# Merged 512-column matmuls, paired rotary scores and a later-ordered second input in a two-layer decoder kernel

## The chip, the cores and the metric

The kernel runs on one core of one Trainium2 chip. The metric is the time of one execution in device microseconds (us); a time without further words is the median of several runs. A profile is one execution, recorded by the hardware profiler. The engines are TensorE (PE in the rows; its weight loads, PEld, overlap its matmuls), VectorE (DVE), ScalarE (ACT), GpSimd (POOL) and SyncE (SP), which here only issues DMAs.

## The reference: what is computed

256 tokens of width 1024 pass two layers; everything is float32.

```python
for i in range(DEPTH):                                   # DEPTH = 2
    hn = rms_norm(h, attn_norm[i])
    if i < N_A_LAYERS:                                   # layer 0
        mix = diff_attention(hn, positions, ...)         # 8 heads, q and k as 2 x 64, v 128, T5 bias
    else:                                                # layer 1
        k_nope, k_pe, v = shared_latent_kv(h, positions, ...)
        mix = mla_attention(hn, ..., k_nope, k_pe, v)    # 16 heads
    h = h + mix
    h = h + conv_gated_ffn(rms_norm(h, ffn_norm[i]), ...)
    h = h + per_layer_embedding(h, p[i], ...)

def mla_attention(...):                                  # one block of 128 queries
    sc = (einsum('bqhd,bkhd->bhqk', qn, k_nope)          # d = 128, per head
          + einsum('bqhr,bkr->bhqk', qp, k_pe)) * scale  # r = 64, one rotary key for all heads
    a = softmax(where(causal_mask, sc, NEG_INF))
    return einsum('bhqk,bkhv->bqhv', a, v)

def conv_gated_ffn(h, w_in, conv_w, conv_b, w_out):      # d_ff = 2816 = 22 x 128
    a, g = split(causal_conv3(h @ w_in) + conv_b)
    return (silu(g) * a) @ w_out
```

The latent key and value come from `rms_norm(h, kv_norm) @ w_dkv` (256 + 64 wide), the queries from `hn @ w_dq` (512 wide) and then `w_uq`.

## The kernel before

**Pairs of numbers.** Each float32 operand is held as a high part and a low part in a shorter format. A product is three matmuls into one accumulator, high times high, high times low and low times high: `mm3`, L199, L200 and L201. The first operand of `T.matmul` (`lhsT`) is the stationary 128x128 tile, the second (`rhs`) the moving one, and its width is the width in columns that the text speaks of. The parts are made by `split`: the high part by ScalarE (L205, or L208 with a gain), the low part by VectorE (L206 or L209).

**Weights.** They lie in units of 128x1024 floats (512 KB) in the order in which they are used. `fetch` (L228) brings a unit by a DMA of SyncE into one of five `st` buffers, `split_unit` casts the high part on ScalarE (L246) and takes the low part on VectorE or on POOL (L247); `share[0]` is the fraction that goes to POOL. The two results stand in a ring of four pairs, `wh` and `wl` (`BUF_W = 4`, L76). A pair is free again when the last matmul that reads it is through.

**Two forms of projection.** In the attentions (`block`, L376) the tokens are stationary: a tile of 128 tokens times 256 columns of a weight unit, for both token tiles (t = 0, 1) into two halves of one accumulator bank of 512 floats. In the feed-forward stages (`wst`, L637) the weight block is stationary and the 256 tokens move, so an output tile is the transposed residual's; `add_h` (L628, L635) adds it. In the second feed-forward product the operand `g`, the gated activation, stands in tiles `og` and `qk` of high and low parts, four or two of them beside each other.

**The stages of the profile.** Start and first block, to some 20 us; layer 0's attention with its projections (`proj_a`, `attn_a`, to 140 us) and output product (to 165); its feed-forward products (165 to 284 and 284 to 345); its embedding (`ple`, to some 378); the second attention's latent (`lps`, 320 columns, then the rotary key `kp`), its query latent (`dps`, 512 columns) to 394; its heads (to 545); the second feed-forward network (560 to 690 and 690 to 752) and the embedding.

**The second attention's input.** The last output tile of `ple` goes through VectorE and ScalarE (`evac`, L844 to L846) and gets the residual added (L628). `b_post` then splits each tile with the latent's gain into `kvs["kvH"]`, `kvs["kvL"]`. The same residual with the attention's own gain is split into `hgH`, `hgL` after `lps` is written out.

**The scores of the second attention** (`s1`, one head at a time, L1155 on): per 128 queries three matmuls of the nope part and three of the rotary part. The rotary queries of two heads lie in the rows 0 to 63 and 64 to 127 of one tile; the rotary key is held twice, each time padded with zeros in the other half (`kpH[e]`), so that each rotary matmul runs over all 128 rows.

**What sets the order.** The program is written as generators: `weave` runs the attention's steps between the projections by an estimate of TensorE's time (`clk`), and `later` delays a step by such an estimate. A scheduler then orders each engine's queue by a simulation of the whole, with priorities that follow the written order; `tc.high_priority` and `tc.issue_after` bend it. Accumulator banks come from four pools A, T, B and C; `BANKS_B` (L80) names, item by item, the pool that a projection of the second attention takes.

## Time and profile before

| | us |
|---|---|
| median of 3 runs | 778.34 |
| lowest and highest of them | 777.44, 778.69 |
| the profiled execution's own time | 777.55 |
| its span | 775.8 |
| TensorE busy | 753.3 |
| VectorE busy | 570.8 |
| ScalarE busy | 485.1 |
| POOL busy | 272.7 |

The span runs from the first to the last instruction of the profiled execution; the rest of its own time, 1.75 us, lies around it. A row of the page or of a group gives line, engine, operation, the output and input tiles by the program's names, the shapes and the count, then busy time and the mean of one in ns, then the idle time of that engine ahead of them with what ended it. A timeline row gives the start in us, the duration, engine, line, tiles and count, and in brackets an idle time ahead of it with its releaser. Matmuls are pipelined: the time of a step is the distance between two starts, and the duration of a row is longer. A row of the table by stretch gives the stretch, its length, the busy time of each engine (and its instructions), the granted clock of TensorE (1.00 is the full one of its two levels), the DMA engines' share and GB/s.

### The profile page before, as it was taken

Reading aid. Unit: us, or ns where it says so; the run is one execution under the profiler, and the core shown is the slowest. Engines: PE = TensorE matmul, PEld = TensorE weight load, DVE = VectorE, ACT = ScalarE, POOL = GpSimd, SP = SyncE. Lnnn points to the kernel's source line nnn. Section 1 sums busy time; section 2 is a strip of 40 time slices with the busy share of each in tenths; the row PEclk is TensorE's granted clock in tenths of the full one; section 3 lists DMA queues with packets and bytes.
Section 4 is the critical chain, followed back from the end, with each engine's and each line's share of the span. In section 5 each row is a group of like instructions: output and inputs, shape, how many; then the busy total and the mean of one; then the engine's idle time right before and its main releaser. Section 6 shows DMA issues by size and latency. Waiting matters only on the chain.

```text
span 775.8 us, 16482 instructions
## 1 busy us (share of the span) xinstructions
PE 753.3 (97%) x6396; PEld 740.0 (95%) x6396; DVE 570.8 (74%) x1141; ACT 485.1 (63%) x1044; POOL 272.7 (35%) x187
## 2 busy tenths in 40 slices
PE   7999999999999999999898999999999999999996
PEld 6999989999999999999798999999999999999996
DVE  6677888568997796546788887876688778875545
ACT  6537876676566665447766876564676666655442
POOL 2655464232332511115616555221342332201231
PEclk9999999999999999999999999999999999999999
DMA  8994444256665576655354133344465566565531
GB/s 293 278 234 160 134 150 136 82 187 181 195 190 177 181 230 216 190 165 176 117 164 166 43 98 112 108 136 135 138 191 189 170 185 195 187 185 174 187 108 55
DMA packets 37519, 127.97 MB, mean 165 GB/s; under 512 B 4672, under 2 KB 6208, under 8 KB 37440
## 3 DMA queue, kind: packets, MB, share of 16 engines
q1 hardware_dynamic: 36432, 126.29, 52.5%
q8 instruction: 50, 0.82, 0.4%
q10 hardware_dynamic: 1008, 0.63, 0.3%
q14 instruction: 29, 0.24, 0.1%
HBM read 125.75 MB, written 1.15 MB: 164 GB/s over the span
## 4 chain that ended last, share of the span: by engine, by line
PE 82%; DVE 8%; ACT 4%; POOL 3%; issue 2%; DMA 1%; SPq 0%; POOLq 0%; ACTq 0%; DVEq 0%
PE pa L199 17%; PE pa L200 17%; PE pa L201 17%; PE pc L201 8%; PE pc L200 8%; PE pc L199 8%; DVE wl L247 2%; POOL wl L247 1%; DVE og L209 1%; ACT wh L246 1%; PE pt L193 1%; POOL s L280 1%; PE pb L482 1%; PE pb L549 1%; PE pc L193 1%
## 5 line engine op out<-in xcount | busy, mean ns | idle before, releaser
L246 ACT CAST wh<-st 128x1024 fp32r<-128x1024 f32 x221 | 230.8, 1049 | 166.5 <-issue 61.2
L247 DVE TENSOR_TENSOR wl<-st,wh 128x1024 fp32r<-128x1024 f32 x160 | 204.6, 1280 | 99.4 <-ACT wh L246 95.8
L247 POOL TENSOR_TENSOR wl<-st,wh 128x1024 fp32r<-128x1024 f32 x61 | 149.6, 2452 | 224.9 <-ACT wh L246 200.2
L201 PE MATMUL pa<-hgH,wl 128*128 128x256 f32 x496 | 140.7, 284 | 0.4 <-POOL wl L247 0.4
L199 PE MATMUL pa<-hgH,wh 128*128 128x256 f32 x496 | 140.4, 283 | 0.0
L200 PE MATMUL pa<-hgL,wh 128*128 128x256 f32 x496 | 140.3, 283 | 0.0
L200 PE MATMUL pa<-og,wh 128*128 128x256 f32 x352 | 99.8, 284 | 0.9 <-DVE og L209 0.9
L199 PE MATMUL pa<-og,wh 128*128 128x256 f32 x352 | 100.2, 288 | 0.1
L201 PE MATMUL pa<-og,wl 128*128 128x256 f32 x352 | 100.1, 285 | 0.0
L199 PE MATMUL pa<-wh,hgH 128*128 128x256 f32 x328 | 93.5, 289 | 4.8 <-DVE d L361 1.7
L304 POOL TENSOR_TENSOR ssq<-ssq,d 128x256 f32<-128x256 f32 x35 | 37.1, 1059 | 172.8 <-ACT d L303 172.4
L201 PE MATMUL pc<-hgH,wl 128*128 128x256 f32 x336 | 95.6, 285 | 1.0 <-DVE wl L247 1.0
L201 PEld LDWEIGHTS pa<-hgH,wl 128*128 128x128 f32 x496 | 95.2, 192 | 0.6 <-POOL wl L247 0.6
L200 PE MATMUL pc<-hgL,wh 128*128 128x256 f32 x336 | 95.1, 283 | 0.1
L199 PEld LDWEIGHTS pa<-hgH,wh 128*128 128x128 f32 x496 | 95.1, 192 | 0.1
L200 PEld LDWEIGHTS pa<-hgL,wh 128*128 128x128 f32 x496 | 95.1, 192 | 0.1
L199 PE MATMUL pc<-hgH,wh 128*128 128x256 f32 x336 | 95.0, 284 | 0.0
L200 PE MATMUL pa<-wl,hgH 128*128 128x256 f32 x328 | 93.4, 286 | 1.5 <-DVE wl L247 0.8
L201 PE MATMUL pa<-wh,hgL 128*128 128x256 f32 x328 | 93.1, 286 | 0.1
L200 PEld LDWEIGHTS pa<-og,wh 128*128 128x128 f32 x352 | 67.7, 192 | 1.1 <-DVE og L209 1.1
L199 PEld LDWEIGHTS pa<-wh,hgH 128*128 128x128 f32 x328 | 62.0, 191 | 6.9 <-DVE d L361 1.9
L199 PEld LDWEIGHTS pa<-og,wh 128*128 128x128 f32 x352 | 67.2, 192 | 0.8 <-ACT og L208 0.3
(304 smaller groups left out, 1913.6 us busy)
## 6 DMA issues: line engine op xcount, KB each, us to landing
st<-in_wall SPq DMA_DIRECT2D x225, 512.0 KB, 3.6
oh<-s SPq DMA_DIRECT2D x24, 128.0 KB, 6.6
hT<-in_x SPq DMA_DIRECT2D x4, 256.0 KB, 5.1
st<-in_wall SPq DMA_DIRECT2D x4, 256.0 KB, 5.3
st<-in_xn SPq DMA_DIRECT2D x2, 512.0 KB, 7.2
d<-in_p SPq DMA_DIRECT2D x2, 256.0 KB, 4.7
out_h<-hT SPq DMA_DIRECT2D x4, 128.0 KB, 1.9
out_h<-hT ACTq DMA_DIRECT2D x4, 128.0 KB, 1.9
```

The source lines that it names most:

```text
L193: lastmm[0] = T.transpose(o, i, ident).ins
L199: T.matmul(ps, lhsT=aH, rhs=bH, start=start, stop=False)
L200: T.matmul(ps, lhsT=aH, rhs=bL, start=False, stop=False)
L201: lastmm[0] = T.matmul(ps, lhsT=aL, rhs=bH, start=False, stop=stop).ins
L209: V.scalar_tensor_tensor(lo, src, scale, f(hi), ALU.mult, ALU.subtract)
L246: A.copy(hi, st)
L247: eng.tensor_sub(lo, st, f(hi))
L280: G.tensor_tensor(dst, src, neghalf[:, :n], ALU.pow)
L304: sqlast[0] = G.tensor_add(sq, sq, t).ins
L482: T.matmul(ps[:, i * 32:(i + 1) * 32], lhsT=lh, rhs=tb[z], start=z == 0, stop=z == 2)
L549: T.matmul(pss[e][:, a:b], lhsT=x[rows, j, t * P:(t + 1) * P], rhs=y[rows, j, :b - a], start=start, stop=stop)
```

## The change

**512 columns in the second feed-forward product.** The high and low parts of `g` now stand side by side, and a new `mm2` multiplies the stationary high part of the weight with both at once, one matmul of 512 columns, then the low part of the weight with the high part, 256 columns, into the first half of the bank. The second half is added to the residual by VectorE ahead of the first. Seven of eight output tiles go this way; the last keeps `mm3`.

**512 columns in the projections.** Query and key weights of the first attention's pairs of heads are laid side by side in one 512-column unit, as are key and value weights of the second, and the rotary queries of four heads beside the nope queries of two of them (`pq_b`). `wide` runs them with one token tile per bank. All four units of a query-key block are held through both token tiles. The order of the second attention's items, its banks and the place from which POOL gets a share are new.

**Rotary scores.** The scores of two heads are computed together. The rotary matmuls use the 64 rows of their own head, written in alternation, the key stands once, and the zeros, POOL's fill and copies are gone.

**The second attention's input.** The splits with the attention's own gain wait for the last split of the latent's input; the last evacuation of the first `ple` has high priority; POOL takes no low parts from there until later.

**The first block.** It now has four units with two halves each, and 512 columns a matmul.

The diff, cut:

```diff
-    order = [("kv", 0), ("kv", 1), ("pe", 0), ("qn", 0), ("qn", 1), ("kv", 2), ("qn", 2), ("pe", 1)]
-    for p in range(3, 8):
-        order += [("kv", p)] + ([("pe", p // 2)] if p % 2 == 0 else []) + [("qn", p)]
-    order.insert(order.index(("qn", 6)) + 1, ("wo", (0, 4)))
+    order = [("kv", 0), ("kv", 1), ("pq", 0), ("qn", 1), ("kv", 2), ("pq", 1), ("kv", 3), ("qn", 3)]
+    for p in range(4, 8):
+        order += [("kv", p), ("qn", p) if p % 2 else ("pq", p // 2)]
+    order.insert(order.index(("pq", 3)) + 1, ("wo", (0, 4)))
...
-BANKS_B = "ABACAACAACAA"
+BANKS_B = "ABACBACACCAA"
 SH_A = 0.5
 SH_FFN = 0.4
 SH_PLE = 0.5
-SH_B0 = 0.5
...
+    def mm2(ps, aH, aL, b, start, stop):
+
+
+        n = b.shape[-1]
+        clk[0] += 3 * max(0.107, n * 0.000427)
+        T.matmul(ps[:, :2 * n], lhsT=aH, rhs=b.rearrange("p c n -> p (c n)"), start=start, stop=False)
+        lastmm[0] = T.matmul(ps[:, :n], lhsT=aL, rhs=b[:, 0], start=False, stop=stop).ins
...
+    for i in range(4):
+        nc.sync.dma_start(hT[:, 2 * i:2 * i + 2], xT[:, 2 * i:2 * i + 2])
+        for st in fetch(2):
+            pass
         first.append(st)
...
+    def wide(t, units, lH, lL, ps):
+
+        for i, u in enumerate(units):
+            for j in range(2):
+                k, c = 2 * i + j, slice(j * 512, (j + 1) * 512)
+                mm3(ps, lH[:, k, t * P:(t + 1) * P], lL[:, k, t * P:(t + 1) * P], u[0][:, c], u[1][:, c], k == 0,
+                    k == 2 * len(units) - 1)
...
+            us = [load_unit() for i in range(4)]
+            for t in range(NT):
                 ps = bankA()
-                us = [(load_unit(), 4) for i in range(2)]
-                block(8, us, S, 0, S, hgH, hgL, ps)
-            yield 1
-            todo.append((s, ps))
-            if p == 0 and s == 0:
-                epsx()
...
+        for s in range(2):
+            later(LAG, lambda s=s, pr=(qk(), qk()): fin(s, *pr))
+        us = [load_unit() for i in range(2)]
+        ps = bankA()
+        block(8, [(u, 4) for u in us], S, 0, S, hgH, hgL, ps)
+        yield 1
+        dH, dL = qk(), qk()
+        for t in range(NT):
+            split(dH[:, t], dL[:, t], ps[:, t * S:(t + 1) * S], xs["r"][:, t:t + 1])
+        QA[p]["v"] = dH, dL
...
-    def add_h(n, ps, post):
+    def add_h(n, ps, post, more=None):
 
         if post:
+            if more is not None:
+                V.tensor_add(hT[:, n], hT[:, n], more)
...
-            mm3(pss[n], u[0][:, b * P:(b + 1) * P], u[1][:, b * P:(b + 1) * P], bH(k), bL(k), k == 0, k == kn - 1)
+                pss[n] = bank()
+            ps, c, p = pss[n], slice(z * P, (z + 1) * P), b(k)
+            if n < wide:
+                mm2(ps, u[0][:, c], u[1][:, c], p, k == 0, k == kn - 1)
+            else:
+                mm3(ps[:, :S], u[0][:, c], u[1][:, c], p[:, 0], p[:, 1], k == 0, k == kn - 1)
             if k == kn - 1:
-                add_h(n, pss.pop(n), post)
-            if b == 7:
+                add_h(n, ps[:, :S], post, ps[:, S:] if n < wide else None)
+                del pss[n]
...
-        run(wst(FFN_OUT_ORDER, lambda k: gH[k], lambda k: gL[k], post, bankW))
+        run(wst(FFN_OUT_ORDER, lambda k: g[k], post, bankW, NK - 1))
...
-                if n == 4:
+                if n == 4 and l == 1:
...
-                evac(*todo.pop(0))
+                if n == NK - 2 and l == 0:
+                    with tc.high_priority():
+                        evac(*todo.pop(0))
+                else:
+                    evac(*todo.pop(0))
...
-        split(kvs["kvH"][n // 4][:, n % 4], kvs["kvL"][n // 4][:, n % 4], ps, col(C_KV + n))
+        kvs["last"] = split(kvs["kvH"][n // 4][:, n % 4], kvs["kvL"][n // 4][:, n % 4], ps, col(C_KV + n))
...
-    share[0] = SH_B0
+    share[0] = 0.0
...
-        split(kvs["hgH"][n // 4][:, n % 4], kvs["hgL"][n // 4][:, n % 4], hT[:, n], col(C_ATTN[1] + n))
-    zer = d_tile(S)
-    G.memset(zer, 0.0)
-    with tc.issue_after(sqlast[0]):
-        for tl in (kpH, kpL):
-            G.tensor_copy(tl[0][64:, :], zer[64:, :])
-            G.tensor_copy(tl[1][:64, :], zer[:64, :])
+        with tc.issue_after(kvs["last"][0]), tc.issue_after(kvs["last"][1]):
+            split(kvs["hgH"][n // 4][:, n % 4], kvs["hgL"][n // 4][:, n % 4], hT[:, n], col(C_ATTN[1] + n))
...
         u = load_unit()
-        ps = bankF()
-        block(2, [(u, 2)], 512, 0, S, ckH, ckL, ps)
-        yield 1.3
-        src = norm_block(ps, 2, P, EPS)
-        ps = bankF()
-        block(2, [(u, 2)], 512, S, S, ckH, ckL, ps)
-        yield 1.3
+        pss = [bankF() for t in range(NT)]
+        for t in range(NT):
+            wide(t, [u], ckH, ckL, pss[t])
+        yield 2.6
...
+    def pq_b(c):
...
+        us = [load_unit() for i in range(2)]
+        pss = []
+        for t in range(NT):
+            pss.append(bankF())
+            wide(t, us, cqH, cqL, pss[t])
+            yield 2.6
+        qn = norm_block(pss, 4, 64, EPS)
+        q_fin(2 * c, norm_block([x[:, S:] for x in pss], 2, P, EPS))
...
+            pss = [bankB() for _ in range(2)]
+
+            def nope(t, a, b, start):
+                for e in range(2):
+                    ts_ = slice(t * P, (t + 1) * P)
+                    mm3(pss[e][:, a:b], q[0][:, e, ts_], q[1][:, e, ts_], k[0][:, e, :b - a], k[1][:, e, :b - a],
+                        start, not start)
+
+            def rotary(t, a, b, start):
+                for z, (x, y) in enumerate(((pe[0], kpH), (pe[0], kpL), (pe[1], kpH))):
+                    for e in range(2):
+                        rows = slice(e * 64, e * 64 + 64)
+                        lastmm[0] = T.matmul(pss[e][:, a:b], lhsT=x[rows, p % 2, t * P:(t + 1) * P],
+                                             rhs=y[rows, :b - a], start=start and z == 0,
+                                             stop=not start and z == 2).ins
+                clk[0] += 0.36
+
+            nope(*QR[0], True)
+            rotary(*QR[0], False)
+            rotary(*QR[1], True)
+            nope(*QR[1], False)
+            for e in range(2):
...
-            if n == 6:
+            if n == 7:
...
-        for s in range(3):
-            natural(wqkv[:, s * 1024 + p * 256:s * 1024 + (p + 1) * 256], 4)
+        q, k, v = (wqkv[:, s * 1024 + p * 256:s * 1024 + (p + 1) * 256] for s in range(3))
+        natural(np.concatenate([q, k], axis=1), 2)
+        natural(v, 4)
...
+    def pq(c):
+        natural(np.concatenate([uq[:, 4 * c:4 * c + 4, P:].reshape(512, 256), qn(2 * c)], axis=1), 2)
...
```

The order in which the instructions stand, at three places. In the second feed-forward product of layer 0 on TensorE, `og` and `qk` hold the activation pair, `wh` and `wl` the weight unit's parts (the rows with `hgH`, `hgL` are the end of the first product); before:

```order
L200 MATMUL pc_4070<-hgL_2344,wh_4103 128x256
L201 MATMUL pc_4070<-hgH_2343,wl_4104 128x256
L199 MATMUL pa_4167<-og_2604,wh_4163 128x256
L200 MATMUL pa_4167<-og_2605,wh_4163 128x256
L201 MATMUL pa_4167<-og_2604,wl_4164 128x256
```

and in the changed kernel, at the change from one output tile to the next:

```order
L207 MATMUL pa_4005<-qk_3795,wh_4085 128x512
L208 MATMUL pa_4005<-qk_3795,wl_4086 128x256
L207 MATMUL pa_4005<-qk_3869,wh_4085 128x512
L208 MATMUL pa_4005<-qk_3869,wl_4086 128x256
L207 MATMUL pc_4103<-og_2407,wh_4085 128x512
L208 MATMUL pc_4103<-og_2407,wl_4086 128x256
```

Two rows stand where three stood. Over the whole queue of TensorE 6373 matmuls become 5681; 256-column ones fall from 5476 to 4092 and 512-column ones rise from 48 to 740.

On TensorE in the second attention's scores, `hgH` and `hgL` are the rotary queries' tiles, `peH` and `peL` the rotary key's, `qk` the nope parts, `pb` the head's bank; before, one head:

```order
L199 MATMUL pb_5882<-hgH_5226,peH_5675 128x128
L200 MATMUL pb_5882<-hgL_5227,peH_5675 128x128
L201 MATMUL pb_5882<-hgH_5226,peL_5676 128x128
L199 MATMUL pb_5882<-qk_5569,qk_5726 128x256
L200 MATMUL pb_5882<-qk_5570,qk_5726 128x256
L201 MATMUL pb_5882<-qk_5569,qk_5727 128x256
L199 MATMUL pb_5882<-hgH_5226,peH_5675 128x256
L200 MATMUL pb_5882<-hgL_5227,peH_5675 128x256
L201 MATMUL pb_5882<-hgH_5226,peL_5676 128x256
```

and in the changed kernel the first pair of heads, and the first head of the second pair:

```order
L1187 MATMUL pb_5494<-hgH_4882,peH_5335 128x128
L1187 MATMUL pb_5495<-hgH_4882,peH_5335 128x128
L1187 MATMUL pb_5494<-hgL_4883,peH_5335 128x128
L1187 MATMUL pb_5495<-hgL_4883,peH_5335 128x128
L192 MATMUL pt_5480<-ident_109,d_5384 128x128 x4
L1187 MATMUL pb_5494<-hgH_4882,peL_5336 128x128
L1187 MATMUL pb_5495<-hgH_4882,peL_5336 128x128
...
L1187 MATMUL pb_5542<-hgH_4882,peH_5335 128x128
L1187 MATMUL pb_5542<-hgL_4883,peH_5335 128x128
L1187 MATMUL pb_5542<-hgH_4882,peL_5336 128x128
L1187 MATMUL pb_5542<-hgH_4882,peH_5335 128x256
```

Seven of the eight pairs of heads alternate like the first, and in three of these another instruction (here four transposes) stands between; one pair has all six of a head behind one another.

On VectorE at the end of layer 0's embedding, `pc` is the last output tile, `rb` the row factor, `prj` the projected embedding, `hT` the residual, and `og` the split tiles of the second attention's two inputs; before:

```order
L844 TENSOR_TENSOR pc_5141<-pc_5141,rb_4991 128x256
L209 SCALAR_TENSOR_TENSOR og_5034<-hT_82,cst_83,og_5032 128x256 x2
L209 SCALAR_TENSOR_TENSOR og_5035<-hT_82,cst_83,og_5033 128x256 x2
L846 TENSOR_TENSOR pc_5141<-pc_5141,prj_2272 128x256
L628 TENSOR_TENSOR pc_5141<-pc_5141,hT_82 128x256
L209 SCALAR_TENSOR_TENSOR og_5031<-pc_5141,cst_83,og_5029 128x256
L247 TENSOR_TENSOR wl_5415<-st_5412,wh_5414 128x1024
```

and in the changed kernel:

```order
L865 TENSOR_TENSOR pc_4797<-pc_4797,rb_4647 128x256
L251 TENSOR_TENSOR wl_5047<-st_5044,wh_5046 128x1024
L867 TENSOR_TENSOR pc_4797<-pc_4797,prj_2075 128x256
L650 TENSOR_TENSOR pc_4797<-pc_4797,hT_82 128x256
L214 SCALAR_TENSOR_TENSOR og_4687<-pc_4797,cst_83,og_4685 128x256
L214 SCALAR_TENSOR_TENSOR og_4690<-hT_82,cst_83,og_4688 128x256 x4
L214 SCALAR_TENSOR_TENSOR og_4691<-hT_82,cst_83,og_4689 128x256 x2
L251 TENSOR_TENSOR wl_5065<-st_5062,wh_5064 128x1024
```

The four splits of `hT` have gone from ahead of the last tile's own steps to behind its split, and a weight's low part has come between. Of the low parts of all weights VectorE has 165 in place of 160, and POOL 54 in place of 61.

## Rows read from the trace of the kernel before

**Rows 1.** The page: busy time of each engine, and the chain by engine.
```profile
PE 753.3 (97%) x6396; PEld 740.0 (95%) x6396; DVE 570.8 (74%) x1141; ACT 485.1 (63%) x1044; POOL 272.7 (35%) x187
...
PE 82%; DVE 8%; ACT 4%; POOL 3%; issue 2%; DMA 1%; SPq 0%; POOLq 0%; ACTq 0%; DVEq 0%
```

**Rows 2.** Busy time by stretch (from:to, length, engines, clock, DMA).
```profile
0.00:20.00 20.00, 15.96 (x96) 13.01 (x97) 13.85 (x51) 13.39 (x27) 5.95 (x15) 1.00 0.83 296
60.00:140.00 80.00, 78.32 (x728) 74.76 (x727) 68.02 (x175) 59.84 (x170) 38.14 (x24) 0.98 0.44 139
284.00:345.00 61.00, 61.00 (x514) 61.00 (x513) 35.53 (x45) 31.28 (x50) 8.09 (x6) 1.00 0.61 192
394.00:432.00 38.00, 34.22 (x280) 32.90 (x278) 30.29 (x56) 26.53 (x80) 15.80 (x10) 1.00 0.46 149
```

**Rows 3.** Timeline of TensorE, 200 to 204 us, first feed-forward product.
```profile
199.75 0.28 PE L199 MATMUL pa<-hgH,wh 128*128 128x256 f32 x1
...
203.59 0.28 PE L201 MATMUL pa<-hgH,wl 128*128 128x256 f32 x1
```

**Rows 4.** Timeline of TensorE, 380 to 396 us, second attention's query latent.
```profile
385.33 0.39 PE L200 MATMUL pc<-wl,og 128*128 128x512 f32 x1
...
391.72 0.39 PE L201 MATMUL pc<-wh,og 128*128 128x512 f32 x1
```

**Rows 5.** The group of line 635, from the groups by tile hT.
```profile
L635 DVE TENSOR_TENSOR hT<-hT,pa x40: 394/416/425, 119.5 to 541.4; 128x256 f32<-128x256 f32 x40
```

**Rows 6.** Timeline of TensorE, 500 to 505 us, one head's rotary scores.
```profile
502.86 0.28 PE L199 MATMUL pb<-hgH,peH 128*128 128x128 f32 x1
...
503.19 0.33 PE L199 MATMUL pb<-qk 128*128 128x256 f32 x1
...
503.61 0.28 PE L199 MATMUL pb<-hgH,peH 128*128 128x256 f32 x1
...
503.96 0.22 PE L201 MATMUL pb<-qk 128*128 128x128 f32 x1
```

**Rows 7.** Timeline of TensorE, first attention: scores on half height, two places.
```profile
65.41 0.95 PE L549 MATMUL pb<-qk 64*128 64x128 f32 x6
66.29 0.39 PE L200 MATMUL pa<-wl,hgH 128*128 128x256 f32 x1
...
70.69 0.28 PE L200 MATMUL pa<-wl,hgH 128*128 128x256 f32 x1
70.90 0.96 PE L549 MATMUL pb<-qk 64*128 64x128 f32 x12
71.78 0.39 PE L201 MATMUL pa<-wh,hgL 128*128 128x256 f32 x1
72.01 0.60 PE L193 MATMUL pt<-ident,d 128*128 128x128 f32 x4
```

**Rows 8.** Timeline of TensorE, 376 to 383 us, end of the embedding.
```profile
377.86 0.28 PE L201 MATMUL pa<-dr,xl 128*128 128x256 f32 x1
380.93 0.42 PE L199 MATMUL pb<-wh,og 128*128 128x320 f32 x1 [2.78 <-ACT og L208]
```

**Rows 9.** Timeline of ScalarE, the same place.
```profile
378.94 1.56 ACT L735 COPY prj<-pa 128x512 f32<-128x512 f32 x3 [2.78 <-DVE pc L846]
380.38 0.50 ACT L208 ACTIVATE og<-pc,cst 128x256 fp32r<-128x256 f32 x1
```

**Rows 10.** Timeline of VectorE, the same place.
```profile
373.81 4.75 DVE L209 SCALAR_TENSOR_TENSOR og<-hT,cst,og 128x256 fp32r<-128x256 f32 x4
378.49 0.42 DVE L846 TENSOR_TENSOR pc<-pc,prj 128x256 f32<-128x256 f32 x1
```

**Rows 11.** The page, costliest groups: the weights' splits.
```profile
L246 ACT CAST wh<-st 128x1024 fp32r<-128x1024 f32 x221 | 230.8, 1049 | 166.5 <-issue 61.2
L247 DVE TENSOR_TENSOR wl<-st,wh 128x1024 fp32r<-128x1024 f32 x160 | 204.6, 1280 | 99.4 <-ACT wh L246 95.8
L247 POOL TENSOR_TENSOR wl<-st,wh 128x1024 fp32r<-128x1024 f32 x61 | 149.6, 2452 | 224.9 <-ACT wh L246 200.2
```

233 lines of the change are left out of this document (103 added, 130 removed).

## The prediction

> **What bounds the kernel now.** I read the busy times of the page first, then busy time by stage, then single rows of TensorE's timeline for the price of one matmul, then the three engines around one wait. The page says that TensorE is busy for 753.3 of 775.8 us with 6396 instructions, and that the chain of work that ended last runs on it for 82% [rows 1]. The stages agree: in a second feed-forward product TensorE is busy for 61.00 of 61.00 us, with VectorE at 35.53 [rows 2]. The second such stage (690 to 752 us) is alike. There only fewer or shorter matmuls shorten the time. In the attentions TensorE is nearly full too, 78.32 of 80 us in the middle of the first one and 34.22 of 38 us at the front of the second, but VectorE is at 68.02 (85%) and 30.29 us (80%) there [rows 2]. So a microsecond saved on TensorE is worth a microsecond in the feed-forward stages, and perhaps less in the attentions.
>
> **Merged matmuls.** Total columns stay the same: one 512-column matmul stands where two 256-column ones with the same stationary tile stood. By the order, 6373 matmuls become 5681, 692 fewer: 2 x 7 x 22 = 308 in the two feed-forward products (seven of eight output tiles), 4 x 8 x 2 x 3 = 192 in the query and key projections of the first attention, 96 in kv and 96 in pq of the second (8 units x 2 k x 2 t x 3, and 4 x 4 x 2 x 3). The price of a 256-column matmul: from 199.75 to 203.59 us 32 steps pass, 3.84 us, 120 ns a step [rows 3]. Of a 512-column one: from 385.33 to 391.72 us, 28 steps of 6.39 us, 228 ns [rows 4]. Two steps become one: 240 - 228 = 12 ns, at about 11 ns where the 256-column step is 119 ns, as in the projections. 308 x 11.8 + 384 x 11 ns = 3.6 + 4.2 = 7.9 us. All of it is on TensorE, and the feed-forward part is on the path that sets the end. The 512-column rows come from the first projection of the second attention, where the wide operand is a weight; that the wide operand is an activation pair in the new product I take to cost nothing more, since a row names no such difference.
>
> The Trainium skill ("TensorE: Matmul & The Clock Gate", Back-to-back issue gap) gives the step as columns divided by 2.4 plus 2.5 ns, so that a merge would save 2.5 ns. By that, 692 merges would save an estimated 1.7 us in place of the 7.9. The trace does not agree: its 120 and 228 ns leave a fixed part of 12 ns, and the sum goes by the rows.
>
> The new product leaves one half to be added, 14 more adds on VectorE at 416 ns [rows 5], 5.8 us. They lie in stages where VectorE is idle for 25 of 61 us [rows 2] and the last output tile is not merged, so the tail gets none: cost nil. If that cover were gone, 5.8 us would be the most.
>
> **Rotary scores.** Per pair of heads the kernel before runs 6 full-height matmuls of 128 columns and 6 of 256. 502.86 to 503.19 us is three of the first, 0.11 each, and 503.61 to 503.96 three of the second, 0.117 to 0.119 each [rows 6]: 6 x .112 + 6 x .119 = 1.39 us. The nearest rows to the new form are the first attention's scores, which alternate between 64-row halves with the same 12 sizes: the twelve take 70.90 to 71.78, 0.88 us, and the ordinary steps before and after them (70.69 to 70.90, 71.78 to 72.01) are each about 0.1 longer than 120 ns, the price of a change of mode: 1.08 us [rows 7]. So an alternating pair saves 0.31. The order shows seven of eight pairs alternating; in three of them a foreign instruction stands in the middle and changes the mode to and fro once more, 0.2 us each. One pair runs head after head: there six half-height matmuls that do not alternate take 65.41 to 66.29, the same 0.88 us, 1.08 with the changes of mode [rows 7], so two heads some 2.15 against 1.39, a loss of 0.76. Sum: 7 x 0.31 - 0.76 - 3 x 0.2 = 0.8 us saved. Bounds: 8 x 0.31 = 2.5 if all is clean, and a loss of 0.9 if a second pair fell out of step and each of the other six had a foreign instruction (6 x 0.11 - 2 x 0.76).
>
> The page "TensorEngine Tiling (Array Packing)" of the Trainium skill (Key Properties) says that a change of tiling mode drains the engine, and its page "TensorE: Matmul & The Clock Gate" (Part 3, Measured speedup vs the span model) puts a pack at one matmul plus about 4 ns for each further tile; an estimate by the latter is half of 1.39 us a pair, 5.6 us in all. The trace shows 1.08, so half is not reached with the mode changes counted.
>
> **The second attention's input.** TensorE runs dry once for long: after 377.86 us it waits 2.78 us for the last split on ScalarE, to start at 380.93 [rows 8]. Going back: ScalarE did three copies (1.56 us) first and the split at 380.38 [rows 9]; VectorE had held the residual's last half back, since four splits of the next input (4.75 us from 373.81, slow beside POOL's weight work) stood ahead of the add at 378.49 [rows 10]. The order of the changed kernel puts these splits behind the last split of the latent's input. In place of 4.75 us stands one weight split, 1.28 us [rows 11]. So the add comes some 3 us sooner, near 375.5, the last split near 377 to 377.6 (the three copies may still stand ahead of it), while TensorE arrives at about 378. The wait that is added holds the eight splits of the next input on ScalarE and VectorE; behind them stand weight work and, on TensorE, the 512-column query projection, which begins six matmuls after the last split is used (six of between 120 and 228 ns, about 0.9 us). Each k there takes 6 x 228 ns = 1.37 us against about 1.19 us (4.75 / 4) for a split at its slowest, so this wait costs nothing after the first split, and the first is ready 1 to 1.5 us after the last one of the latent: up to 0.6 us, within the bounds below. What is late next is the latent's first weights, on VectorE: two to three more weight splits are now there, as POOL gives them up (POOL's take 2452 ns each [rows 11]). I take 2.0 us of gain, with 0 (the copies or those splits are late by as much) and 2.8 (the wait is gone) as bounds.
>
> **Front of the second attention.** TensorE idles 38 - 34.22 = 3.8 us here [rows 2]. The merged blocks hold a full bank a token tile until norms and splits on VectorE have read it; in the old form a bank was given back after 256 columns of each tile. The bank sequence is reordered, POOL gets its weight share one item later, and VectorE has some two more weight splits (2.6 us) in a stage at 80%. Both ends are open: the idle 3.8 us could go, and the same could come again. I take a cost of 1.0, nearer to zero than to 3.8, as VectorE has 7.7 us idle here and two splits of 1.28 us would fill a third of it.
>
> **First attention and start.** About 15 more reads of 256 columns replace fewer wider ones on VectorE at 85%; I take 0.5 us of the 2.1 us of TensorE's merges in that stage as not paid. At the start, the first block grows from 48 matmuls of 120 ns to 48 of 228 ns, 10.9 us, while its weights and inputs, 3 MB, need 10.1 us at the 296 GB/s of the first 20 us, in which TensorE is idle for 4.0 us [rows 2]. Work that came later now fills gaps, but a later transfer can leave a new one: I take 0, between -1.5 (part of the 4.0 idle filled) and +2.0 (half of it again).
>
> **Sum.** The profiled execution took 777.55 us, 0.79 below the median of 778.34. 777.55 - 7.9 - 0.8 - 2.0 + 1.0 + 0.5 = 768.35; with the 0.79 the forecast is 769.1 us. Its own range, by the bounds, is 766 to 772.
>
> **Rivals.** A: *VectorE sets the pace in both attentions.* Then merges there and rotary give nothing, the feed-forward and the input order stay: 777.55 - 3.6 - 2.0 + 1.0 + 0.79 = 773.7. For it: 85% and 80% busy [rows 2]. Against: TensorE has only 1.7 us idle in the 80.
>
> B: *Everything pays*: 7.9 + 2.5 + 2.8 + 1.5, no cost at the front: 777.55 - 14.7 + 0.79 = 763.6. For it: the front's idle time and POOL, which is eased. Against: VectorE takes on work.
>
> C: *A merged matmul costs what its two halves cost* when the wide operand is an activation pair: only the other terms are left, 777.55 - 0.8 - 2.0 + 1.0 + 0.5 + 0.79 = 777.0, no change that can be told. Against it: 28 equal steps of 228 ns. The skill's formula above, 1.7 us from the merges, would stand near it, at an estimated 775.3.
>
> D: *The ring of four weight pairs stalls TensorE, and the kernel is slower.* A merged query-key block holds all four pairs through two passes of its four units. The pair freed next needs a cast (1049 ns) and a split on POOL (2452 ns) [rows 11], 3.5 us, before its next unit is there. Three such blocks with two handovers each are six places, 21 us if nothing covers them. What covers them: three more units of a pass, 3 x 6 x 228 ns = 4.1 us, and the attention's matmuls woven in. The gains are 9.2 us net, so it ends slower from 9.2 of the 21 on; with 12 it is 769.1 + 12 = 781.1.
>
> **How the numbers follow.** Chances: forecast 0.57, A 0.17, B 0.14, C 0.05, D 0.07. The range that holds the first three, 762 to 774.5, leaves out 0.12 and the edges. About 0.2% (1.6 us) is what a measurement of this kernel can tell from no change. Faster: the forecast, A and B, 0.88; same: C and a trace of D, 0.06; slower: the rest of D, 0.06.
>
> **What would show it.** Some 692 fewer rows on TensorE; steps of 120 and 228 ns in the new feed-forward product, which ends about 1.8 us shorter, twice; alternating rotary rows of some 1.1 us for 12, one pair of heads at 2 us; the wait of 2.78 us near 378 gone or below 1; six to eight microseconds less busy time on TensorE. The forecast is wrong if the 512-column step is above 235 ns, if new waits for weight splits stand at the query-key blocks (D), or if TensorE's idle time in the attentions grows by what its busy time falls (A).

## The result

| | median us | lowest and highest | runs |
|---|---|---|---|
| before | 778.41 | 777.44, 778.69 | 4 |
| changed | 790.11 | 788.04, 790.43 | 4 |

The changed kernel is slower: ratio 1.0147, 95% interval 1.0127 to 1.0166; the medians lie 11.7 us apart. The forecast was 769.1 us with a range of 762.0 to 774.5. The profiled execution of the changed kernel took 790.33 us, with a span of 788.5, against 777.55 and 775.8 before: 12.7 us more.

The page of the changed kernel, with the busy time of the engines and the chain by engine, answers to [rows 1]:

```profile
PE 757.6 (96%) x5704; PEld 705.9 (90%) x5704; DVE 578.8 (73%) x1182; ACT 487.3 (62%) x1052; POOL 254.1 (32%) x175
...
PE 77%; DVE 8%; ACT 6%; DMA 3%; POOL 3%; issue 2%; SPq 0%; POOLq 0%; DVEq 0%; ACTq 0%
```

The 692 matmuls are gone, and yet TensorE is busy for 4.3 us more, and idle for 30.9 us of its span where it was idle for 22.5. Busy time by stretch answers to [rows 2] (columns as there; stretches after the first lie later in the program's work by some microseconds, since the kernel runs late):

```profile
0.00:20.00 20.00, 17.83 (x71) 14.53 (x72) 12.16 (x37) 11.96 (x22) 1.92 (x13) 1.00 0.89 322
60.00:140.00 80.00, 75.76 (x589) 66.47 (x587) 62.48 (x162) 55.98 (x158) 36.28 (x22) 0.96 0.39 132
284.00:345.00 61.00, 61.00 (x368) 54.04 (x367) 43.06 (x64) 34.03 (x54) 6.31 (x5) 1.00 0.65 206
394.00:432.00 38.00, 33.35 (x161) 26.72 (x160) 28.93 (x68) 22.96 (x72) 11.59 (x8) 0.96 0.44 139
432.00:545.00 113.00, 105.10 (x779) 95.35 (x780) 88.13 (x242) 74.15 (x235) 48.33 (x45) 0.98 0.31 99
```

The last of these stretches, in the kernel before:

```profile
432.00:545.00 113.00, 111.95 (x949) 111.02 (x948) 87.95 (x230) 72.89 (x218) 46.45 (x44) 1.00 0.34 107
```

The feed-forward stage is full, as before. The attentions have more idle time, and their mean granted clock is lower: 0.96, 0.96 and 0.98 in the three stretches, against 0.98, 1.00 and 1.00.

**Where the time went.** Both programs do the same number of columns, so I laid the two timelines of TensorE over each other at equal columns done. The table gives by how many microseconds a kernel is later (+) or earlier at the point that the kernel before reaches at the time on the left. The last two columns are runs of the next section. A value is good to some 0.4 us.

| place, us of before | changed | first projections alone | second projections alone |
|---|---|---|---|
| 26.7, after the first block | -0.1 | -1.8 | +0.8 |
| 68.0, first scores | 0.0 | -3.9 | 0.0 |
| 104.6 | +3.3 | -0.6 | +0.2 |
| 141.9, end of the first attention | +8.2 | +6.3 | +0.2 |
| 279.2, second feed-forward product | +8.2 | +6.2 | +0.2 |
| 342.8, its end | +7.2 | +6.2 | +0.2 |
| 393.3, second input and query latent | +4.7 | +7.5 | +1.7 |
| 475.0, second attention | +14.6 | +8.5 | +8.2 |
| 545.8, its end | +14.0 | +8.5 | +6.7 |
| 768.8, end | +12.9 | +8.5 | +6.7 |

So the feed-forward products and the second input pay about what they should (-1.0 twice, -2.5), and both attentions lose, 8 and 9 to 10 us. That is where the whole loss lies.

The idle time in the attentions, by waits (line waited for, total us, times, longest). The changed kernel from 394 to 565 us, and from 60 to 145 us:

```profile
PE pa L198 <- DVE qk L212: 3.1, 2, 1.6
PE pt L192 <- DVE d L365: 2.3, 1, 2.3
PE pc L192 <- DVE dr L212: 2.0, 1, 2.0
PE pt L192 <- DVE qk L214: 1.2, 2, 0.7
...
PE pc L192 <- DVE ex L591: 1.6, 1, 1.6
PE pc L198 <- DVE dr L212: 1.3, 1, 1.3
```

The same of the kernel before, 390 to 551 us, where the sum is below 5:

```profile
PE pa L199 <- DVE d L361: 1.7, 1, 1.7
PE pa L199 <- DVE qk L206: 1.4, 1, 1.4
```

Most of the new waits stand in front of the attention's own steps (transposes of normalized queries, of the weights `ex`, products with `dr`), not in front of projections. Behind some of them the clock fell. TensorE's granted clock (the third column from the right) by stretch, of the changed kernel and then of the kernel before:

```profile
115.00:119.00 4.00, 3.64 (x17) 3.56 (x18) 3.85 (x5) 3.19 (x9) 3.83 (x3) 0.57 0.47 176
136.00:140.00 4.00, 3.83 (x20) 3.51 (x20) 2.22 (x7) 0.95 (x2) 0.70 (x1) 0.57 0.43 138
422.00:427.00 5.00, 3.42 (x10) 2.57 (x10) 3.52 (x12) 1.15 (x8) 1.93 (x2) 0.66 0.25 95
443.00:447.00 4.00, 4.00 (x22) 3.77 (x21) 3.20 (x16) 2.15 (x12) 3.58 (x6) 0.57 0.00 0
```

```profile
113.00:117.00 4.00, 4.00 (x24) 3.90 (x20) 2.47 (x12) 3.17 (x10) 2.52 (x2) 0.57 0.73 289
```

A mean of 0.57 in 4 us says that most of it ran at the lower of the two levels, 1.2 GHz, and that 4 x 0.43 = 1.7 us of full-speed work was lost. The changed kernel has four such stretches between 20 and 770 us, the kernel before has one: 5.1 us. The Trainium skill ("TensorE: Matmul & The Clock Gate", Part 1) has the lower level follow idle time; the rows agree in part: three of the four stretches stand behind waits of 1.3 to 2.4 us, the fourth behind two of 0.9 and 0.7 us. But a wait of this length does not always bring one: behind the 2.78 us of [rows 8] the kernel before stayed at 1.00, and in the run with the merged product alone the clock fell behind the same wait, of 2.78 us again. The two stretches, before and in that run:

```profile
380.00:386.00 6.00, 5.07 (x26) 4.44 (x27) 2.46 (x4) 5.83 (x18) 3.75 (x5) 1.00 0.13 51
378.00:384.00 6.00, 5.48 (x21) 4.53 (x21) 2.78 (x4) 4.93 (x16) 4.10 (x6) 0.72 0.12 36
```

The merges of the projections did save time on TensorE. Two rows of the changed kernel, eight steps of 512 columns apart:

```profile
418.55 0.39 PE L198 MATMUL pa<-wh,hgH 128*128 128x512 f32 x1
...
420.40 0.40 PE L200 MATMUL pa<-wh,hgL 128*128 128x512 f32 x1
```

That is 231 ns a step, against two of 120: some 3.6 us for 384 merges. With 8.4 us more idle, 5.1 us less clock and some 4.0 us more for the first attention's scores (below), less 2.0 in the feed-forward products, 0.2 in the rotary scores (below) and these 3.6, 11.7 of the 12.7 us are accounted for.

### The profile page after: what moved, and what is told of

Read it like the earlier page. It is cut to its first block, busy times and chain, and to the rows that moved or that the text cites. A ratio compares the mean times of both kernels' runs of the same rounds, so it can differ in the third digit from the quotient of the medians.

```text
span 788.5 us, 15089 instructions
## 1 busy us (share of the span) xinstructions
PE 757.6 (96%) x5704; PEld 705.9 (90%) x5704; DVE 578.8 (73%) x1182; ACT 487.3 (62%) x1052; POOL 254.1 (32%) x175
## 4 chain that ended last, share of the span: by engine, by line
PE 77%; DVE 8%; ACT 6%; DMA 3%; POOL 3%; issue 2%; SPq 0%; POOLq 0%; DVEq 0%; ACTq 0%
PE pa L198 13%; PE pa L199 13%; PE pa L200 13%; PE pc L200 6%; PE pc L199 6%; PE pc L198 6%; PE pa L207 6%; PE pc L207 3%; PE pa L208 3%; DVE wl L251 2%; DMA oh<-s 2%; POOL s L283 2%; ACT wh L250 2%; PE pc L208 2%; PE pb L571 1%
## 5 line engine op out<-in xcount | busy, mean ns | idle before, releaser
L250 ACT CAST wh<-st 128x1024 fp32r<-128x1024 f32 x219 | 228.3, 1049 | 148.3 <-issue 49.1
L251 POOL TENSOR_TENSOR wl<-st,wh 128x1024 fp32r<-128x1024 f32 x54 | 131.3, 2431 | 201.1 <-ACT wh L250 180.1
L198 PE MATMUL pa<-wh,hgH 128*128 128x512 f32 (+1 forms) x202 | 71.6, 362 | 4.2 <-DVE qk L212 3.1
L199 PE MATMUL pa<-wl,hgH 128*128 128x512 f32 (+1 forms) x202 | 72.0, 356 | 2.3 <-DVE wl L251 2.3
L283 POOL TENSOR_TENSOR s<-s,neghalf 128x4 f32<-128x4 f32 (+2 forms) x30 | 45.1, 1504 | 85.2 <-DVE s L357 57.9
L200 PE MATMUL pa<-wh,hgL 128*128 128x512 f32 (+1 forms) x202 | 71.5, 354 | 0.0
L200 PEld LDWEIGHTS pc<-hgH,wl 128*128 128x128 f32 x336 | 64.5, 192 | 1.4 <-DVE wl L251 1.4
L199 PEld LDWEIGHTS pc<-hgL,wh 128*128 128x128 f32 x336 | 64.5, 192 | 0.3 <-DVE hgL L214 0.3
L198 PEld LDWEIGHTS pc<-hgH,wh 128*128 128x128 f32 x336 | 64.4, 192 | 0.1
L198 PE MATMUL pa<-og,wh 128*128 128x256 f32 x208 | 60.2, 293 | 1.0 <-DVE hT L657 0.5
L199 PE MATMUL pa<-og,wh 128*128 128x256 f32 x208 | 59.9, 289 | 0.0
```

What stands on the lines that cost most here:

```text
L198: T.matmul(ps, lhsT=aH, rhs=bH, start=start, stop=False)
L199: T.matmul(ps, lhsT=aH, rhs=bL, start=False, stop=False)
L200: lastmm[0] = T.matmul(ps, lhsT=aL, rhs=bH, start=False, stop=stop).ins
L250: A.copy(hi, st)
L251: eng.tensor_sub(lo, st, f(hi))
L283: G.tensor_tensor(dst, src, neghalf[:, :n], ALU.pow)
```

## The experiments

Every ratio is against the kernel before on the same chip. The edits are shown by their main lines.

**One part alone.** Four kernels take one part of the change each.

```diff
-        run(wst(FFN_OUT_ORDER, lambda k: gH[k], lambda k: gL[k], post, bankW))
+        run(wst(FFN_OUT_ORDER, lambda k: g[k], post, bankW, NK - 1))
```

> The kernel before with the merged second feed-forward product alone. By the price of the forecast (12 ns a merge, 308 merges) 778.4 - 3.6 = 774.8 us. By the rows of the changed kernel, where the 512-column step is 233 ns and each product came out about 1.0 us shorter, 778.4 - 2.0 = 776.4. If the added work on the vector engine cost something, 778.4 or more.

775.07 us against 777.85, ratio 0.9967 (0.9955 to 0.9980). At equal columns each of the two products gains 1.0 us, as in the changed kernel, and the interval (1.6 to 3.5 us) holds these 2.0. For the rest of the 2.8 the profile shows no cause: its curve runs ahead by over 1 us in the first attention, where nothing is edited, and is back by 390 us (the next run is 1.7 us ahead there, with nothing of it edited either).

```diff
+        with tc.issue_after(kvs["last"][0]), tc.issue_after(kvs["last"][1]):
+            split(kvs["hgH"][n // 4][:, n % 4], kvs["hgL"][n // 4][:, n % 4], hT[:, n], col(C_ATTN[1] + n))
```

> The kernel before with the ordering of the second attention's input alone (the splits behind the last latent split, the high priority, no weight parts on POOL there). Forecast: 2.0 us less, 776.4; by the trace of the changed kernel, where the stretch from 341 to 394 us before is some 2.3 us shorter, 776.1. If the gain there is given back at the front of the second attention, since POOL does less, 778.4.

775.68, ratio 0.9972 (0.9961 to 0.9984). At equal columns it gains 2.1 us up to 382.5 us, and has given 2.2 back by 401 us: the wait moved. A microsecond and a half came back later in the second attention.

```diff
+            for t in range(NT):
                 ps = bankA()
+                wide(t, us, hgH, hgL, ps)
```

> The kernel before with the merged query and key projections of the first attention alone, its first block with them. Theory one (the merged block itself delays what follows it): the 8.1 us that the changed kernel lost between 68 and 142 us come back, 786.5 us. Theory two (the loss came from the order that the scheduler made of all parts together): 776 to 779.

786.22, ratio 1.0114 (1.0096 to 1.0132): 8.4 us lost by the merge alone, 6.3 of them by the end of its own stage. The rest comes later in this profile, at some 384 and 430 us, with two stretches of low clock (386 to 391 and 434 to 439 us of its own time, 0.66 each, 1.7 us of full-speed work) behind waits that the kernel before has too. Theory one.

```diff
+        pss = [bankF() for t in range(NT)]
+        for t in range(NT):
+            wide(t, [u], ckH, ckL, pss[t])
```

> The kernel before with the merged projections of the second attention alone (kv, pq, the new order of items and banks), rotary scores still at full height, one head at a time. Theory one: the merged blocks lose there, about 10 to 12 us (9 in the changed kernel, where the rotary rows gave 2.7 back), 788 to 790 us. Theory two (the scores of two heads at once hold two banks and cause the waits): 776 to 779.

784.27, ratio 1.0090 (1.0076 to 1.0104): 6.4 us lost, less than expected, but theory one again; the scores still went head by head.

**The scores out of alternation.** The rotary rows were forecast from the first attention's scores, where twelve matmuls of two halves alternate [rows 7]. In the changed kernel these scores themselves came apart. TensorE's timeline there:

```profile
69.56 0.95 PE L571 MATMUL pb<-qk 64*128 64x128 f32 x6
70.44 0.50 PE L200 MATMUL pa<-wh,hgL 128*128 128x512 f32 x1
70.78 0.39 PE L198 MATMUL pa<-wh,hgH 128*128 128x512 f32 x1
71.01 0.40 PE L199 MATMUL pa<-wl,hgH 128*128 128x512 f32 x1
71.34 0.95 PE L571 MATMUL pb<-qk 64*128 64x128 f32 x6
72.22 0.50 PE L200 MATMUL pa<-wh,hgL 128*128 128x512 f32 x1
```

Six matmuls of one half take 0.88 us, as long as the twelve of two alternating halves took in [rows 7], and then six more follow elsewhere. Of 95 neighbours among the 96 score matmuls 45 alternated before, 28 in the changed order. All score rows together went from 8.8 to 12.1 us; with the ordinary steps ahead of and behind each run of them, which are about 0.1 us longer (71.01 to 71.34 is 0.33 where a step is 0.23), from some 11.0 to 15.0. The order alone showed this. A constraint that holds them in alternation:

```diff
+                        with (tc.issue_after(prev[0]) if prev else ExitStack()):
+                            prev = [T.matmul(pss[e][:, a:b], lhsT=x[rows, j, t * P:(t + 1) * P],
+                                             rhs=y[rows, j, :b - a], start=start, stop=stop).ins]
```

> The merged projections of the first attention as before, and the twelve score matmuls of a head's two halves held in alternation by an order constraint. Theory one (the scheduler took the halves apart, because the second bank of a pair comes free later, and this costs about 3 of the 8.4 us): 783 us. Theory two (it is only the late start of the attention's steps, and the scores would wait for their bank anyway): 786 us, no change against the merged projections alone.

782.75, ratio 1.0053 (1.0035 to 1.0071): 3.5 of the 8.4 us back. In the whole changed kernel, with the same three lines:

> The changed kernel with the first attention's scores held in alternation. If what it gave with the merged projections alone (3.5 us) adds, 790.1 - 3.5 = 786.6 us. If the other parts take it up, 790.

786.06, ratio 1.0095 (1.0062 to 1.0128), 4 us back (780.80 in the profiled execution, 786.0 to 786.7 in the other three).

**Is it the last pair, or the ring?**

```diff
+        elif p in WIDE_A:
...
+WIDE_A = (0, 1, 2)
```

> The merged projections of the first attention for the first three of four pairs of heads, the last pair's query and key again in two 256-column blocks. Theory one (the merged block gives query and key of a pair later, and what is late at the end has no projection left to hide it): the idle time of the last part, some 4 us, goes, 782 us. Theory two (each merged block costs alike): 8.4 / 4 = 2.1 less, 784 us.

784.35, ratio 1.0064 (1.0031 to 1.0096): 1.9 us back, nearer to theory two, though the interval holds both.

```diff
-BUF_W = 4
+BUF_W = 5
```

> The merged projections of the first attention with alternating scores (782.75 us) and a ring of five weight pairs instead of four. If the block that holds all four pairs delays what follows (rival D of the forecast), 779 to 780 us. If not, 782 to 783.

782.79, ratio 1.0064 (1.0048 to 1.0080), the same as with four pairs. The ring, rival D, has no part in it that can be told.

**The second attention's parts.** Key-value units merged, the queries as before:

```diff
-        ps = bankF()
-        block(2, [(u, 2)], 512, 0, S, ckH, ckL, ps)
...
+        pss = [bankF() for t in range(NT)]
+        for t in range(NT):
+            wide(t, [u], ckH, ckL, pss[t])
```

> The kernel before with only the key-value projections of the second attention merged (both banks of an item are held until the key's norm and the value's split are both through; before, one bank held the key and one the value). Theory one (the time for which a bank is held decides): most of the 6.4 us that all merged projections of the second attention cost, 781 to 784 us. Theory two (the merged rotary and nope queries and their order do it): 777 to 778.5.

781.10, ratio 1.0035 (1.0019 to 1.0051): 3.1 us lost, half of what all merged projections lose there. Both theories are half right. The rotary scores in pairs:

```diff
-        def s1(h):
+        def s1(p):
...
+            nope(*QR[0], True)
+            rotary(*QR[0], False)
+            rotary(*QR[1], True)
+            nope(*QR[1], False)
```

> The kernel before with the rotary scores on half height for two heads at once, alone. By the forecast 0.8 us less, 777.0. By the parts so far (-2.8, -2.2, +8.4, +6.4 make +9.8 of the +12.3 measured) some 2.5 us more, 780.

779.10, ratio 1.0007 (0.9991 to 1.0022): no change that can be told. A pair that alternates, in the changed kernel:

```profile
501.00 0.42 PE L200 MATMUL pb<-qk 128*128 128x128 f32 x2
501.35 0.33 PE L1187 MATMUL pb<-hgH,peH 64*128 64x128 f32 x2
...
502.23 0.38 PE L198 MATMUL pb<-qk 128*128 128x256 f32 x1
502.46 0.28 PE L199 MATMUL pb<-qk 128*128 128x256 f32 x1
```

0.88 us for twelve, and all rotary steps of the stage fell from 11.2 to 8.6 us (8.4 in this run). But the ordinary steps around them grew: 501.00 to 501.35 is 0.35 for two of 0.11, 502.23 to 502.46 is 0.23 for one of 0.12. Such changes of mode stand at both ends of 12 runs in the changed kernel and of 10 here, 2.5 and 2.1 us in all. So the rotary scores cost 11.0 us of TensorE's time in the changed kernel and 10.4 here, against 11.2: 0.2 and 0.8 us saved.

**Does TensorE's work set the end of an attention?** Here a part of the work is left out: in the projections of the first attention's last two pairs the third product, and in another run the same in the second attention from the fourth pair on.

```diff
+        mm = mm3 if third else mm3_two
...
+                block(8, us, S, 0, S, hgH, hgL, ps, third=p < 2)
```

> The kernel before without the third product (low part of the tokens times high part of the weights) in the query, key and value projections of the first attention's last two pairs of heads: 96 matmuls of 120 ns less, 11.5 us of TensorE's work in the middle of that stage. The results lack that product. Theory one (the chain of the attention's own steps from the first scores to the last head sets the end of the stage): the projections end some 11 us sooner, and the stage hardly, 775 to 778 us. Theory two (TensorE's work sets it, as the forecast took it): 778.0 - 11.5 = 766.5 us.

781.98, ratio 1.0047 (1.0026 to 1.0068). With 11.5 us less to do, the kernel is 3.8 us **slower**. This is the run that decides. Three rows each, for the kernel before and for this one: TensorE's last projection matmul, and VectorE's first read of a score and last split of a head's output. Before:

```profile
106.03 0.28 PE L201 MATMUL pa<-wh,hgL 128*128 128x256 f32 x1
```

```profile
67.06 0.28 DVE L557 CUSTOM_DVE_ANT_0 ex<-pb,bias 128x128 f32<-128x128 f32 x1
142.05 0.48 DVE L209 SCALAR_TENSOR_TENSOR og<-pc,gq,og 128x256 fp32r<-128x256 f32 x1 [1.79 <-ACT og L208]
```

Without the third product:

```profile
94.00 0.28 PE L206 MATMUL pa<-wl,hgH 128*128 128x256 f32 x1
```

```profile
67.97 0.28 DVE L563 CUSTOM_DVE_ANT_0 ex<-pb,bias 128x128 f32<-128x128 f32 x1
145.47 0.48 DVE L214 SCALAR_TENSOR_TENSOR og<-pc,gq,og 128x256 fp32r<-128x256 f32 x1 [3.14 <-ACT og L213]
```

The projections end 12 us sooner. The chain of the eight heads starts 0.9 us later than before and takes 77.5 us in place of 75.0. The freed time became waits, from 56 to 150 us of this kernel:

```profile
PE pc L193 <- DVE da L366: 4.2, 2, 3.2
PE pb L555 <- DVE sa L563: 2.7, 1, 2.7
PE pt L193 <- DVE qk L214: 2.3, 1, 2.3
```

That is some 9 us of waits against 1.6 before, and in this stage 6.8 us of full-speed work lost to the low clock against 1.7. The edit also changed the order: in it only 12 of the 95 neighbours among the scores alternate, and the score rows take 10.9 us in place of 8.8. One of them, six of one half in 0.88 us:

```profile
66.63 0.95 PE L555 MATMUL pb<-qk 64*128 64x128 f32 x6
67.51 0.38 PE L205 MATMUL pa<-wh,hgH 128*128 128x256 f32 x1
```

These two, 5.1 and 2.1 us, can explain that the kernel got slower, so the 3.8 us are not the price of less work. They do not save theory two: even with both taken off the 11.5, 4.3 us should have been gained. The same chain in the changed kernel (66.03 to 149.84, 83.8 us) and with alternating scores (70.28 to 147.14, 76.9 us):

```profile
66.03 0.29 DVE L579 CUSTOM_DVE_ANT_0 ex<-pb,bias 128x128 f32<-128x128 f32 x1 [0.56 <-PE pb L571]
149.84 0.48 DVE L214 SCALAR_TENSOR_TENSOR og<-pc,gq,og 128x256 fp32r<-128x256 f32 x1 [1.65 <-ACT og L213]
```

```profile
70.28 0.28 DVE L572 CUSTOM_DVE_ANT_0 ex<-pb,bias 128x128 f32<-128x128 f32 x1
147.14 0.48 DVE L209 SCALAR_TENSOR_TENSOR og<-pc,gq,og 128x256 fp32r<-128x256 f32 x1 [1.83 <-ACT og L208]
```

In the kernel with alternating scores, the end of the last head is 5.1 us later than before, and the whole stage is 5.1 us later at equal columns; in the changed kernel 7.8 and 8.2. The end of the chain is the end of the stage. With the alternation held, 3.2 of the 5.1 us lie ahead of the chain's first row and 1.9 in the chain; in the changed kernel the chain starts 1.0 us sooner and takes 8.8 us longer. The second attention:

```diff
-        block(4, [(u, 4)], S, 0, S, cqH, cqL, ps)
+        block(4, [(u, 4)], S, 0, S, cqH, cqL, ps, third=p < 3)
```

> The kernel before without the third product in the key-value and nope-query projections of the second attention from the fourth pair of heads on: 80 matmuls of 120 ns less, 9.6 us. The results lack that product. Theory one (the chain of that attention's steps sets the end): 775 to 778 us. Theory two (TensorE's work): 768.4 us.

776.82, ratio 0.9982 (0.9972 to 0.9992): 1.3 of 9.6 us. The second attention is the same kind of stage.

**What paces the chain?** First the weights' splits in the queues of VectorE and POOL: the same amount of TensorE's work left out by another product, and with it the low parts of twelve weight units.

```diff
+    def load_high():
+        hi, lo = ring_pair()
+        A.copy(hi, next(fetch()))
+        return hi, hi
```

> The kernel before without the second product (high part of the tokens times low part of the weights) in the projections of the first attention's last two pairs of heads, and without the low parts of these twelve weight units: the same 96 matmuls, 11.5 us, are left out of TensorE's work as in the run without the third product (782.0 us), and besides six splits of 1.28 us on the vector engine and six of 2.45 on POOL. The results lack that product. Theory one (the attention's chain waits in the queues of the vector engine and POOL): clearly below that run and below the kernel before, 771 to 775 us. Theory two (the chain is paced by its own steps and banks, not by these queues): 779 to 782 us.

780.58, ratio 1.0044 (1.0020 to 1.0068). Twelve splits fewer change nothing that can be told (1.4 us against the run without the third product, whose interval overlaps): no sign that these splits pace it. Whether the other work in the same queues does, this run can't show. Then the idle gap itself, filled:

```diff
+            for i in range(18 if h in (4,) else 0):
+                T.matmul(pw[:, :S], lhsT=vF[:, 0, :P], rhs=vF[:, 0], start=True, stop=True)
```

> The merged projections of the first attention with alternating scores (782.75 us), and 18 more matmuls of 256 columns, 2.2 us, whose results are overwritten, ahead of the fifth head's weight transposes, where TensorE waited for 2.61 us; the rest of its order stays. In that kernel's profile the granted clock stood at its lower level for most of 108 to 123 us, behind that wait, 6.8 us of full-speed time. Theory one (the wait itself is a small part of its price, the larger is the clock behind it): the stretch of low clock shrinks or goes, 777 to 780 us. Theory two (the chain sets the end, and the clock follows without a price): 782 to 783 us, or 2 more.

782.98, ratio 1.0072 (1.0051 to 1.0093), no change that can be told. The fill missed the gap. TensorE with alternating scores, and with the fill:

```profile
106.26 0.50 PE L199 MATMUL pa<-og,wh 128*128 128x256 f32 x2 [1.32 <-ACT og L208]
109.37 0.90 PE L193 MATMUL pc<-ident,ex 128*128 128x128 f32 x3 [2.61 <-DVE og L209]
```

```profile
111.06 3.61 PE L593 MATMUL pc<-qk 128*128 128x256 f32 x18 [2.61 <-DVE og L209]
114.47 0.84 PE L193 MATMUL pc<-ident,ex 128*128 128x128 f32 x3
```

The filling matmuls depend on no result of the head, write the same bank and have the same wait of 2.61 us ahead of them: so the wait is for a bank of pool C, which VectorE's split of an earlier output (`og`, L209) still reads. The 2.2 us of work that were added behind it did not lengthen the chain: in this profile it takes 74.9 us (72.08 to 146.98) against 76.9. There the low clock behind the gap cost 1.7 us of full-speed work in place of 6.8 (mean clock 0.995 against 0.988 over the span). The median can't show what that is worth: of the six executions only two had such a clock (0.995 and 0.994, at 782.88 and 782.42 us), the other four had 0.988 to 0.990, as the run without filling (0.988 to 0.992). The same for each of the last four heads, in two places:

```diff
+            for i in range(8 if h >= 4 else 0):
+                T.matmul(pw[:, :S], lhsT=vF[:, 0, :P], rhs=vF[:, 0], start=True, stop=True)
...
+            for i in range(8 if h >= 4 else 0):
+                T.matmul(po[:, :S], lhsT=vH[:, 0, :P], rhs=vH[:, 0], start=True, stop=True)
```

> The same kernel with 8 such matmuls ahead of the weight transposes and 8 ahead of the products with the values for each of the last four heads, 64 in all, 7.7 us of added work. Theory one (what the clock loses in these gaps is worth more than the added work that does not fit into them): 779 to 782 us. Theory two: 782.75 plus what does not fit into the 4.7 us of waits, 786 to 790 us.

788.65, ratio 1.0131 (1.0109 to 1.0152), as theory two: what does not fit into a gap is paid. One of the bank's users moved:

```diff
-            to_T(st.pop(("o", h)), oH[h // 4][:, h % 4:h % 4 + 1], oL[h // 4][:, h % 4:h % 4 + 1], gq[:, 2:3],
-                 bankC)
+            to_T(st.pop(("o", h)), oH[h // 4][:, h % 4:h % 4 + 1], oL[h // 4][:, h % 4:h % 4 + 1], gq[:, 2:3])
```

> The merged projections of the first attention with alternating scores (782.75 us), and the transposes of the heads' outputs go to the bank of pool T instead of one of the two of pool C, through which the weights' transposes, the products with the values and these outputs pass head after head. In that kernel the longest wait, 2.61 us, was for a bank of pool C that the vector engine still read. Theory one (the two banks of pool C pace the chain): that wait goes, 778 to 780 us. Theory two (the chain is as late by its other steps): 782 to 783 us.

786.78, ratio 1.0118 (1.0087 to 1.0149): 4 us worse. The wait of 2.61 us is gone from this run's list, but others stand in its place, 4.9 us in all as before. The bank they moved to is a single one that the queries' and keys' transposes use. So theory one is not shown by this run, and it is not refuted either: the pools hold eight banks (A three, T one, B two, C two), and no run gave the chain a third one of its own.

**A version of the parts that pay.** The merged product with the second input's order, and then also the first block and the held alternation:

```diff
+                mm2(ps, u[0][:, c], u[1][:, c], p, k == 0, k == kn - 1)
...
+        with tc.issue_after(kvs["last"][0]), tc.issue_after(kvs["last"][1]):
```

> The kernel before with the merged second feed-forward product and the second input's order, the two parts that gained alone: if they add up, 778.0 - 2.8 - 2.2 = 773.0 us.

776.96, ratio 0.9986 (0.9976 to 0.9996): 1.1 us, less than each part alone, and not the 5.0 expected. At equal columns it is 3.8 us ahead at 390 us and has lost that by 475 us, in the second attention.

```diff
+WIDE_A = (0,)
...
+                        with (tc.issue_after(prev[0]) if prev else ExitStack()):
```

> The same with the first block merged (only the first pair's query and key) and the first attention's scores held in alternation. If the chain of the attention sets its stage, an earlier first score and shorter score rows start and shorten it: 769 to 771 us. If the start gives nothing to the chain, 773 as without these two.

776.67, ratio 0.9977 (0.9966 to 0.9988), a miss as well: the chain of heads, from 66.77 to 145.12 us in this profile, did not get shorter. The merged product alone, 775.07 us, has the lowest ratio of all runs and beats both kernels; its interval overlaps those of this run and of the second input's order.

## Why the prediction was wrong

- **The merged product in the feed-forward stage: right in place, mis-sized.** The term was 12 ns a merge. A wide step and the narrow one behind it, in the changed kernel:

```profile
306.02 0.40 PE L207 MATMUL pc<-og,wh 128*128 128x512 f32 x1
...
309.55 0.39 PE L207 MATMUL pc<-qk,wh 128*128 128x512 f32 x1
```

  Ten pairs take 3.53 us, 353 ns each, against three times 119.3 = 358 ns in the old product of that stage (59.9 us for 502 steps of the timeline). That is some 5 ns a merge here; 1.0 us a product and not 1.8, over 154 merges, is 6 to 7. The 512-column step of [rows 4] stood among its like; between 256-column steps it takes 233 to 235 ns. The adds on VectorE cost nothing, as said.
- **Merged projections: the step that failed.** The term "384 x 11 ns" put 4.2 us on TensorE, near its measured size (some 3.6), and counted it as time saved; only 0.5 was taken back in the first attention. It rests on the sentence that TensorE "is nearly full too". It was full because projection matmuls filled whatever the chain of heads left open, and not because its work set the end: with 11.5 us less of that work the stage did not end sooner. The bound from below was zero (rival A: the merges "give nothing"). There was no reason to stop at zero, since the merge changes when banks come free and in which order the steps stand; it cost 8.4 and 6.4 us. With every other term at its bad end (rotary scores 1.7 us, second input 2.0, front 2.8, start 2.0) the sum would still be 777.6 us; this term had no bad end at all.
- **The front of the second attention** was taken at +1.0, between -3.8 and +3.8. From 415.8 to 475 us the changed kernel lost 10.4 us. Half of what merged projections lose there comes with the key-value units alone, as a bank that is read by two slower users would do; this was argued in the forecast, and the 3.1 us were measured, but that the held bank is their cause was not shown.
- **The rotary scores: right in kind, and nothing in the time.** 0.8 us were forecast, changes of mode counted, and TensorE's rows gave 0.8 in the run with this part alone and 0.2 in the changed kernel. An alternating pair stands at 0.88 us and some 0.2 for the changes of mode, the forecast's 1.08. In the time the run alone shows nothing that can be told. The Trainium skill's pack rule ("TensorE: Matmul & The Clock Gate", Part 3), half of 1.39 us a pair, an estimated 5.6 us in all, is not what the rows show.
- **The second input: right.** 2.0 was the term, 2.1 to 2.5 the gain up to the query latent, and the wait of 2.78 us is gone. The run with this part alone showed that the gain is short-lived: the next stage takes it back, so that the 2.2 us which that run gained in the time can't be put down to it.
- **The start: right**, 0 forecast, -0.1 at 26.7 us.
- **The order was read in three places and not in a fourth.** I counted how many pairs of the second attention's scores would alternate, and did not count the first attention's, which the change does not touch in its text. Its scores lost their alternation, 3.5 to 4 us.
- **The rivals.** A named the place. B did not occur. C is half true, at 5 to 7 of 12 ns. D forecast slower, for a cause that the run with five pairs does not bear out.

**What stays open.** What paces the chain of heads: the weights' splits and the ring made no difference that can be told, one wait is known to be for a bank, and a test of the banks failed. Why the merged key-value and query units cost 6.4 us in the second attention was not tested beyond the split into 3.1 and the rest. And what share the clock has: 5.1 us of low clock more are in the changed kernel's profile. In the 102 executions of the kernel before that were taken beside the runs, the time rises by some 5.8 us for each 0.01 of mean clock lost, where 7.8 would be the full price; two executions at 0.991 took 781.9 us on average, three at 0.998 took 776.7. By this estimate the changed kernel's clock (0.987 to 0.991 against 0.995) would be some 3.5 of its 11.7 us. But waits come ahead of the low clock and cost time themselves, so these numbers go together without showing which is the cause.

## What to carry to other kernels

An engine that is busy for 97% is the bound only if less of its work makes the stage shorter; where other work is woven in to fill it, leave out some of that filler and look whether the stage ends sooner, before pricing a change by instructions saved, and look at the order of that test too, since it may have lost something else. When a change makes an engine's tile larger, ask how long its accumulator is then held by the readers (that this is the price here was argued, not shown), and do not put the lower bound of its worth at zero. Where a scheduler sets the order, count the pattern you rely on (here alternating halves) in every stage of the new order, not in the edited one.
